# A decoder layer with three token mixers: five of the dilated mixer's seven projections per head computed as seven-block products

## The chip, the cores and the metric

One core of a Trainium2 chip runs the whole program. The metric is device time in microseconds of one execution. A core's engines are called PE (TensorE, with its weight load PEld), ACT (ScalarE), DVE (VectorE), POOL (GpSimd) and SP (SyncE, which issues most transfers). Each works through its own list in order; a semaphore holds an instruction until what it needs is there.

## The reference, cut to what matters

`x` has 512 tokens of width 2048. One projection of the normalised and modulated input `u` gives all columns of the layer, and a part of them feeds the dilated mixer (C): three groups of eight heads, 128 columns per head and group, and a gate `c_z`.

```
u = rms_norm(x, norm_w) * (1.0 + scale) + shift
proj = u @ w_in                       # 512 x 2048 times 2048 x 23552
for g, (w, d) in enumerate(((128, 1), (512, 4), (2048, 16))):
    s = q[g] @ k[g].T * 128 ** -0.5   # a window of w, every d-th token
    o[g], lse[g] = softmax(s) @ v[g], logsumexp(s)
o_c = sum(softmax(lse)[g] * o[g])     # per token and head
y_c = (o_c * silu(c_z)) @ w_proj_c    # A (differential) and B (retention) alike
merged = sigmoid(g_a) * y_a + sigmoid(g_b) * y_b + sigmoid(g_c) * y_c
out = rms_norm(x + gate * (merged @ w_out), final_norm_w)
```

## The kernel before, in words

**Products.** A float32 product is made of three matmuls on a high and a low part of each operand (`mm3`, L157 to L160). A plain projection of 128 output columns (`proj`, L162) loads two weight halves of 512 KB on SP (`w_load`, L130, tile `wr`, three buffers), splits each by a copy on ACT (L146, `wh`) and a subtraction on DVE (L147, `wl`), and runs 16 row blocks times 3 matmuls, 48 in all, of 128x512.

**Stages.** The start phase forms the modulation, `u`, and some gate columns; POOL does the low parts of those weights there (L278). Then comes the phase of seven-block products (L496 to L698), then the eight heads of mixer C (L942 to L974), the C gate phase, mixers A and B with theirs, and the output product.

**The phase of seven-block products.** A unit (`unit_jobs`, L555) is the product of `u` with 1024 weight columns, cut into 2x2 blocks and computed with seven block products in place of eight. It has 14 jobs: P1 (2), P2 (2), R3 (2) and eight sum jobs. A job loads one 1 MB raw tile `xr` (SP, two jobs ahead, three buffers), splits it (`xh` on ACT, L506; `xl` on DVE, L507), forms sums on DVE in the sum jobs (L592), and multiplies (`block_mul`). For values a job has 24 matmuls of 128x512. For the gates (`fm=True`, output with features on partitions) it has 48 of 128x256. The results are collected in the steps `keep` (L574, ACT copies P1 to tile `p1` and R3 to tile `r3`), `p2_done` (L580, DVE writes tile `c`), `done_z` (L610), `done_s` (L616 and L617) and `done_rest`. Tiles `c`, `r3`, `s` and `z` have one buffer each. Each is written to DRAM by a DMA that POOL issues (`put_values`, L643; `put_gates`, L655, behind a sigmoid on ACT), so the same tile of the next unit waits for that DMA to land.

There are nine units: three of C's values, A's and B's values, and four of gates: 126 jobs. PE, ACT and DVE instructions of this phase are kept in program order (`pin`, L152). POOL's instructions are not: a scheduler places them.

**The heads of C.** Each head runs seven plain projections (q and k for each group, and z). Scores, softmax, transposes and values are placed between their two halves (`mid=`). Values come back from DRAM for two heads at a time (`v_load`, L210, into the `wr` buffers). The softmax sums cross DRAM (`bounce`), and POOL reads back the weights `wtb`. POOL also forms nine columns of gate bias (`gate_bias_load`, L707): per column four loads of 256 KB into one buffer `bw` (L711), each with a multiplication by the shift and two or three additions (L713 to L719). PE adds up the partitions (L724).

Of the kernel before, what the change touches and what calls it, by code (L numbers as in the profile page):

```python
# [64 lines left out]
def hybrid_kernel(ctx, tc, x, c, w_in, w_pa, w_pb, w_pc, w_out, w_ada, b_ada, norm_w, lam,  # L65
# [32 lines left out]


# [34 lines left out]

    def w_half(src, k0, c0, rot=False, tiles=None, low=dve):

        r, h, l = tiles or w_load(src, k0, c0)
# [7 lines left out]
        else:  # L145
            act.copy(h, r)  # L146
            low.tensor_sub(l, r, h.bitcast(F32))  # L147
        return h, l

    pinned = [False]  # L150

    def pin(instr):  # L152

        if pinned[0]:
            tc.keep_in_program_order(instr)
# [40 lines left out]
    def split_pairs(pool, tag, src):  # L196

        t = pool.tile([P, 4, 2, P], F32R, tag=tag, name=tag)
        act.copy(t[:, :, 0, :], src)
        dve.tensor_sub(t[:, :, 1, :], src, t[:, :, 0, :].bitcast(F32))  # L200
        return t
# [448 lines left out]
    def put_gates(g, b0):  # L650
        def put(t, half, cc):
            def f():
# [6 lines left out]


    units = [unit_jobs(w_in, c0, put_values(unit), early=unit == 3)
             for unit, c0 in ((2, C_V), (3, C_V + 1024), (4, C_V + 2048), (0, A_V), (1, B_V))]
    units += [unit_jobs(w_in, g + b0 * P, put_gates(g, b0), fm=True) for g in (G_A, G_B) for b0 in (0, 8)]
    jobs = units[1][0] + units[0][0] + units[0][1] + units[1][1]
# [26 lines left out]
    pinned[0] = False  # L691
    for f in later:
        f()
    for f in deferred:
        f()
    wx_es.close()
# [3 lines left out]
    wp_es, wp = open_pool("wp2", "left", reuse_waits="tile")  # L700
# [4 lines left out]


    def gate_bias_load(pool, db):  # L707
        br = pool.tile([P, P], F32, tag="br", name="br", bufs=2)
        for q in range(4):
            r = pool.tile([P, 4, P], F32, tag="bw", name="bw", bufs=1)  # L710
            nc.gpsimd.dma_start(out=r, in_=w_in[q * 512:(q + 1) * 512, G_C + db * P:G_C + (db + 1) * P]  # L711
                              .rearrange("(j p) c -> p j c", p=P))
            nc.gpsimd.tensor_mul(r, r, sh[:, q * 4:q * 4 + 4].unsqueeze(2).broadcast_to([P, 4, P]))  # L713
            nc.gpsimd.tensor_add(r[:, 0:2, :], r[:, 0:2, :], r[:, 2:4, :])
            if q == 0:
                nc.gpsimd.tensor_add(br, r[:, 0, :], r[:, 1, :])
            else:
                nc.gpsimd.tensor_add(r[:, 0, :], r[:, 0, :], r[:, 1, :])
                nc.gpsimd.tensor_add(br, br, r[:, 0, :])  # L719
        return br  # L720
# [87 lines left out]
    def bias_step():  # L808
        while bias_open:
            gate_bias_sum(*bias_open.pop(0))  # L810
# [520 lines left out]
```

## Time and profile before

| | us |
|---|---|
| median of three runs | 2669.22 (2666.35 to 2669.69) |
| the profiled execution | 2663.64 |
| its span | 2661.9 |
| start phase, up to the first seven-block job | 0 to 238.6 |
| seven-block products, nine units | 238.6 to 961 |
| C's first head, up to the next turn | 961 to 1055.2 |
| one C head after that | 84.7 |
| what follows the C heads | from 1647.6 |

The span runs from the first to the last instruction of the profiled execution. In the rows further down, a timeline row has the start in us, the duration in us, the engine, the line in the kernel, the operation, out<-in, sizes, and in brackets how long the engine had been idle and what released it. A row "x36 | 287.0, 1271" of the groups gives the count, the busy us and the mean ns of one. A window row has the stretch, its length, and for PE, PEld, DVE, ACT and POOL the busy us with the number of instructions, then PE's granted clock, DMA share and GB/s. A row of the DMA issues gives count, KB each, and us from issue to landing.

### The profile page before, as it was taken

The numbers are of one execution on the slowest core, as the hardware profiler recorded it, in microseconds if no ns is written. First come the engines' busy times: TensorE is split into PE (matmuls) and PEld (weight loads), VectorE is DVE, ScalarE is ACT, GpSimd is POOL, SyncE is SP. The second block draws the span as 40 slices with busy tenths as digits, with TensorE's granted clock in tenths as the row PEclk, the third lists the DMA queues.
The fourth block names the chain that finished last, engine by engine and source line by source line (L and its number), as shares of the span: only waits on it lengthen the run. The fifth ranks groups of instructions, "written<-read, shape, count | busy, mean of one in ns | idle before, by whom it ended". The sixth has DMA issues, their size and how long they took to land.

```text
span 2661.9 us, 33296 instructions
## 1 busy us (share of the span) xinstructions
PE 2568.5 (96%) x13091; PEld 2184.6 (82%) x13091; DVE 1689.0 (63%) x2427; ACT 1058.6 (40%) x1431; POOL 269.6 (10%) x271
## 2 busy tenths in 40 slices
PE   6999999999999999999999999999999989999898
PEld 5777778888999988888888888788888768878778
DVE  7994888777778754444443444357667457676674
ACT  4233433333334433233333333246666235653222
POOL 3332000000000024122214200000000000000000
PEclk9999999999999999999999999999999999999999
DMA  9776666666666655344445443542333563336862
GB/s 345 252 273 227 231 208 226 225 221 214 197 207 220 208 154 147 96 119 120 114 119 123 106 121 109 175 142 82 93 88 92 171 194 104 98 99 210 299 222 103
DMA packets 414017, 449.47 MB, mean 169 GB/s; under 512 B 24786, under 2 KB 308132, under 8 KB 412708
## 3 DMA queue, kind: packets, MB, share of 16 engines
q1 hardware_dynamic: 384388, 396.91, 47.6%
q0 software_dynamic: 9760, 33.59, 4.2%
q10 hardware_dynamic: 19712, 16.85, 1.9%
q8 instruction: 102, 1.67, 0.3%
q14 instruction: 55, 0.45, 0.1%
HBM read 406.86 MB, written 40.44 MB: 168 GB/s over the span
## 4 chain that ended last, share of the span: by engine, by line
PE 74%; DVE 11%; DMA 8%; ACT 3%; issue 2%; SPq 0%; POOL 0%; ACTq 0%; DVEq 0%
PE pj L158 15%; PE pj L160 15%; PE pj L159 15%; PE at L159 8%; PE at L160 8%; PE at L158 8%; DVE acc L318 3%; DMA gpr<-part 2%; DMA gwa<-in_w_ada_dram 1%; DVE xl L507 1%; DMA gsg<-g 1%; DMA xr<-in_w_in_dram 1%; DMA part<-gsg 1%; DMA xr<-ud 1%; DVE xr L592 1%
## 5 line engine op out<-in xcount | busy, mean ns | idle before, releaser
L158 PE MATMUL pj<-uh,wh 128*128 128x512 f32 x1552 | 611.9, 394 | 7.1 <-ACT wh L146 4.8
L160 PE MATMUL pj<-uh,wl 128*128 128x512 f32 x1552 | 608.0, 392 | 7.3 <-DVE wl L144 4.6
L159 PE MATMUL pj<-ul,wh 128*128 128x512 f32 x1552 | 606.7, 391 | 0.0
L147 DVE TENSOR_TENSOR wl<-wr,wh 128x1024 fp32r<-128x1024 f32 x226 | 287.0, 1271 | 392.0 <-ACT wh L146 364.6
L146 ACT CAST wh<-wr 128x1024 fp32r<-128x1024 f32 x228 | 239.2, 1051 | 516.7 <-PE pj L159 365.7
L506 ACT CAST xh<-xr 128x2048 fp32r<-128x2048 f32 x126 | 240.7, 1910 | 365.0 <-PE at L160 152.5
L507 DVE TENSOR_TENSOR xl<-xr,xh 128x2048 fp32r<-128x2048 f32 x126 | 288.8, 2292 | 125.4 <-ACT xh L506 124.6
L160 PEld LDWEIGHTS pj<-uh,wl 128*128 128x128 f32 x1552 | 292.5, 188 | 70.3 <-DVE wl L144 5.5
L158 PEld LDWEIGHTS pj<-uh,wh 128*128 128x128 f32 x1552 | 293.0, 189 | 65.1 <-ACT wh L146 5.0
L159 PEld LDWEIGHTS pj<-ul,wh 128*128 128x128 f32 x1552 | 292.8, 189 | 58.1
L592 DVE TENSOR_TENSOR xr<-xr 128x512 f32<-128x512 f32 x288 | 198.8, 690 | 12.3 <-DMA xr<-in_w_in_dram 5.1
L158 PE MATMUL at<-yh,wh 128*128 128x512 f32 x336 | 131.8, 392 | 5.9 <-DVE gsg L777 5.0
L159 PE MATMUL at<-yl,wh 128*128 128x512 f32 x336 | 131.5, 391 | 0.0
L160 PE MATMUL at<-yh,wl 128*128 128x512 f32 x336 | 131.5, 391 | 0.0
L160 PE MATMUL at<-fh,xl 128*128 128x256 f32 x384 | 108.9, 284 | 0.7 <-DVE xl L507 0.7
L158 PE MATMUL at<-fh,xh 128*128 128x256 f32 x384 | 108.7, 283 | 0.0
L159 PE MATMUL at<-fl,xh 128*128 128x256 f32 x384 | 108.7, 283 | 0.0
L158 PE MATMUL at<-wh,mh 128*128 128x512 f32 (+1 forms) x256 | 93.1, 369 | 6.2 <-DVE res L1252 3.8
L159 PE MATMUL at<-wl,mh 128*128 128x512 f32 (+1 forms) x256 | 94.9, 371 | 0.2
L160 PE MATMUL at<-wh,ml 128*128 128x512 f32 (+1 forms) x256 | 94.5, 369 | 0.0
L278 POOL TENSOR_TENSOR wl<-wr,wh 128x896 fp32r<-128x896 f32 x32 | 77.3, 2421 | 136.5 <-ACT wh L277 127.3
L159 PE MATMUL at<-xl,fh 128*128 128x512 f32 x224 | 88.8, 396 | 2.1 <-DVE xl L507 1.8
(419 smaller groups left out, 5035.4 us busy)
## 6 DMA issues: line engine op xcount, KB each, us to landing
wr<-in_w_in_dram SPq DMA_DIRECT2D x196, 512.0 KB, 3.9
xr<-in_w_in_dram SPq DMA_DIRECT2D x144, 512.0 KB, 4.5
xr<-in_w_in_dram SPq DMA_DIRECT2D x54, 1024.0 KB, 5.1
wa<-in_w_ada_dram SPq DMA_DIRECT2D x20, 1024.0 KB, 9.1
wr<-in_w_out_dram SPq DMA_DIRECT2D x32, 512.0 KB, 4.6
gwa<-in_w_ada_dram SPq DMA_DIRECT2D x32, 512.0 KB, 4.8
wr<-in_w_in_dram SPq DMA_DIRECT2D x32, 448.0 KB, 6.3
wb<-in_w_ada_dram SPq DMA_DIRECT2D x12, 1024.0 KB, 9.3
```

What stands on the lines that cost most here:

```text
L146: act.copy(h, r)
L147: low.tensor_sub(l, r, h.bitcast(F32))
L158: pin(nc.tensor.matmul(ps, lhsT=ah, rhs=bh, start=start, stop=False))
L159: pin(nc.tensor.matmul(ps, lhsT=ah, rhs=bl, start=False, stop=False))
L160: pin(nc.tensor.matmul(ps, lhsT=al, rhs=bh, start=False, stop=stop))
L278: nc.gpsimd.tensor_sub(l, r, h.bitcast(F32))
L318: dve.scalar_tensor_tensor(out=acc, in0=wa[:, j, :], scalar=sc[:, k:k + 1], in1=acc, op0=ALU.mult, op1=ALU.add)
L506: pin(act.copy(h, r))
L507: pin(dve.tensor_sub(l, r, h.bitcast(F32)))
L592: pin(dve.tensor_add(r[:, o, :], r[:, o, :], r[:, a, :]))
```

## The change

Of the seven projections of a C head, q1, k1, q2, k2 and q3 are computed for all heads as five more units of the seven-block kind (features on partitions, as the gates), and written to DRAM (`qk_dram`) by `put_raw`. A's and B's value units move behind them, so the phase has 14 units, 196 jobs. k3 and z stay plain projections.

- A head reads its five operands back from DRAM in `raw_load` tiles: two operands of 256 KB per tile, tag `wr`, the three buffers that the weight halves use as well. Values are now read per head. `head_inputs` of the next head stands behind z; `head_values` stands behind k3.
- The head's other work stands around the two projections: the previous head's turn, the first scores and scores(1) at the middle of k3; the previous head's values behind k3; the first turn and scores(2) at the middle of z.
- `wtb` has a tile of its own, and its DMA is issued right after the write of the sums.
- The gate bias leaves the C heads. It is cut into 72 pieces (`bias_piece`: a load of 128 KB into one buffer `bw`, a multiplication, one or two additions, all on POOL), whose code stands one per job in jobs 16 to 87 of the seven-block phase. The nine columns go to DRAM (`br_dram`), and SP reads one per head (L838).
- The two weight halves of the first k3 are split between the last steps of the seven-block phase.

```diff
+    QK = [C_Q, C_K, C_Q + 1024, C_K + 1024, C_Q + 2048]
+    qk_dram = [dram.tile([8, P, S], F32, tag=f"qk{i}", name=f"qk{i}") for i in range(len(QK))]
+    br_dram = dram.tile([NF + NM, P, P], F32, tag="brd", name="brd")
...
+        if tiles is not None and len(tiles) == 2:
+            return tiles
...
-            act.copy(h, r)
-            low.tensor_sub(l, r, h.bitcast(F32))
+            pin(act.copy(h, r))
+            pin(low.tensor_sub(l, r, h.bitcast(F32)))
...
+    def put_raw(dst):
+        def put(t, half, cc):
+            b = cc // P
+            nc.gpsimd.dma_start(out=dst[b:b + 4, :, half * 256:half * 256 + 256].rearrange("b p t -> p b t"),
+                                in_=t.rearrange("p q (a t) -> p (q a) t", a=2))
+        return put
...
+    def bias_piece(n):
+        db, q = divmod(n, 8)
+        if q == 0:
+            bias_tiles[db] = wxp.tile([P, P], F32, tag="br", name="br")
+        br = bias_tiles[db]
+        r = wxp.tile([P, 2, P], F32, tag="bw", name="bw")
+        nc.gpsimd.dma_start(out=r, in_=w_in[q * 256:(q + 1) * 256, G_C + db * P:G_C + (db + 1) * P]
+                          .rearrange("(j p) c -> p j c", p=P))
+        nc.gpsimd.tensor_mul(r, r, sh[:, q * 2:q * 2 + 2].unsqueeze(2).broadcast_to([P, 2, P]))
+        if q == 0:
+            nc.gpsimd.tensor_add(br, r[:, 0, :], r[:, 1, :])
+        else:
+            nc.gpsimd.tensor_add(r[:, 0, :], r[:, 0, :], r[:, 1, :])
+            nc.gpsimd.tensor_add(br, br, r[:, 0, :])
+        if q == 7:
+            nc.gpsimd.dma_start(out=br_dram[db], in_=bias_tiles.pop(db))
...
-             for unit, c0 in ((2, C_V), (3, C_V + 1024), (4, C_V + 2048), (0, A_V), (1, B_V))]
+             for unit, c0 in ((2, C_V), (3, C_V + 1024), (4, C_V + 2048))]
     units += [unit_jobs(w_in, g + b0 * P, put_gates(g, b0), fm=True) for g in (G_A, G_B) for b0 in (0, 8)]
+    units += [unit_jobs(w_in, c0, put_raw(dst), fm=True) for c0, dst in zip(QK, qk_dram)]
+    units += [unit_jobs(w_in, c0, put_values(unit)) for unit, c0 in ((0, A_V), (1, B_V))]
...
-    pinned[0] = False
+        if 2 * HJ <= i < 2 * HJ + 8 * (NF + NM):
+            bias_piece(i - 2 * HJ)
+    wx_es.close()
+    wp_es, wp = open_pool("wp2", "left", reuse_waits="tile")
+    loads = [w_load(w_in, half * 1024, C_K + 2048) for half in range(2)]
+    entry = []
+    for tiles in loads:
+        entry.append(w_half(w_in, 0, 0, tiles=tiles))
+        later.pop(0)()
     for f in later:
         f()
-    for f in deferred:
-        f()
-    wx_es.close()
+    pinned[0] = False
...
-    def gate_bias_load(pool, db):
-        br = pool.tile([P, P], F32, tag="br", name="br", bufs=2)
-        for q in range(4):
-            r = pool.tile([P, 4, P], F32, tag="bw", name="bw", bufs=1)
-            nc.gpsimd.dma_start(out=r, in_=w_in[q * 512:(q + 1) * 512, G_C + db * P:G_C + (db + 1) * P]
-                              .rearrange("(j p) c -> p j c", p=P))
-            nc.gpsimd.tensor_mul(r, r, sh[:, q * 4:q * 4 + 4].unsqueeze(2).broadcast_to([P, 4, P]))
-            nc.gpsimd.tensor_add(r[:, 0:2, :], r[:, 0:2, :], r[:, 2:4, :])
-            if q == 0:
-                nc.gpsimd.tensor_add(br, r[:, 0, :], r[:, 1, :])
-            else:
-                nc.gpsimd.tensor_add(r[:, 0, :], r[:, 0, :], r[:, 1, :])
-                nc.gpsimd.tensor_add(br, br, r[:, 0, :])
-        return br
...
-    bias_todo, bias_open = list(range(NF + NM)), []
+    bias_todo = list(range(NF + NM))
     def bias_step():
-        while bias_open:
-            gate_bias_sum(*bias_open.pop(0))
-        bias_more()
-    def bias_more():
         if bias_todo:
             db = bias_todo.pop(0)
-            bias_open.append((db, gate_bias_load(cp, db)))
+            br = cp.tile([P, P], F32, tag="br", name="br", bufs=2)
+            nc.sync.dma_start(out=br, in_=br_dram[db])
+            gate_bias_sum(db, br)
...
+            ctx_["wtb"] = cp.tile([P, 2, S], F32, tag="wtb", name="wtb")
+            nc.gpsimd.dma_start(out=ctx_["wtb"], in_=ctx_["bounce"].partition_broadcast(P))
...
-            wtb = cp.tile([P, 2, S], F32, tag="e23", name="wtb")
-            nc.gpsimd.dma_start(out=wtb, in_=ctx_["bounce"].partition_broadcast(P))
-            ctx_["p"], ctx_["wtb"] = ps, wtb
+            ctx_["p"] = ps
...
+    def raw_load(*srcs):
+        r = wp.tile([P, 2, S], F32, tag="wr", name="wr", bufs=3)
+        for i, (src, view) in enumerate(srcs):
+            nc.sync.dma_start(out=view(r[:, i, :]), in_=src)
+        return r
...
+    def head_inputs(hd):
+        got = []
+        for g in range(2):
+            r = raw_load((qk_dram[2 * g][hd], same), (qk_dram[2 * g + 1][hd], same))
+            got.append((split(cp, "q", r[:, 0, :], scale=dh_scale, view=perm if g else None, bufs=2),
+                        split_pairs(cp, "kc", perm(r[:, 1, :]) if g else tiles4(r[:, 1, :]), bufs=2)))
+        return got
+    def head_values(hd):
+        srcs = [(v_dram[2][:, hd * P:(hd + 1) * P].rearrange("(t p) c -> p t c", p=P), tiles4)]
+        srcs += [(v_dram[2 + g][:, hd * P:(hd + 1) * P].rearrange("(i r) c -> i r c", r=4), tiles4) for g in (1, 2)]
+        rs = [raw_load((qk_dram[4][hd], same), srcs[0]), raw_load(*srcs[1:])]
+        q3 = split(cp, "q", rs[0][:, 0, :], scale=dh_scale, view=perm, bufs=2)
+        vs = []
+        for g in range(3):
+            src = tiles4(rs[(g + 1) // 2][:, (g + 1) % 2, :])
+            vh = cp.tile([P, NT, P], F32R, tag=f"v{g}h", name="vh")
+            vl = cp.tile([P, NT, P], F32R, tag=f"v{g}l", name="vl")
+            act.copy(vh, src)
+            dve.tensor_sub(vl, src, vh.bitcast(F32))
+            vs.append((vh, vl))
+        return q3, vs
...
     left = [None, None]
+    inputs = head_inputs(0)
     for hd in range(8):
-        bias_step()
         e1 = cp.tile([P, NT, 256], F32, tag="e1", name="e1")
         st = cp.tile([P, 4, 4], F32, tag="st", name="st", bufs=2)
-        q = split(cp, "q", proj(C_Q + hd * P, mid=left[0]), scale=dh_scale)
-        kc = split_pairs(cp, "kc", proj(C_K + hd * P, mid=left[1]).rearrange("p (r i) -> p r i", r=4))
         p0 = [cp.tile([P, 4, 256], F32R, tag=f"p0{x}", name=f"p0{x}") for x in "hl"]
         e23 = cp.tile([P, 4, 256], F32, tag="e23", name="e23")
         first_scores, first_turn, scores, turn, values, weigh, finish = c_head(hd, e1, e23, st, p0)
-        cq, ck = C_Q + hd * P, C_K + hd * P
-        ps = proj(cq + 1024, mid=lambda: first_scores(*q, kc))
-        q2 = split(cp, "q", ps, scale=dh_scale, view=perm)
-        ps = proj(ck + 1024, mid=first_turn)
-        kc2 = split_pairs(cp, "kc", perm(ps))
-        ps = proj(cq + 2048, mid=lambda: scores(1, *q2, kc2))
-        q3 = split(cp, "q", ps, scale=dh_scale, view=perm)
-        kc3 = split_pairs(cp, "kc", perm(proj(ck + 2048)))
-        if hd == 4:
-            bias_more()
-        if hd % 2 == 0:
-            vs = [v_load(cp, 2 + g, hd * P, f"v{g}", strided=g > 0) for g in range(3)]
-        sz = silu(cp, proj(C_Z + hd * P, mid=lambda: scores(2, *q3, kc3)))
+        (q1, kc1), (q2, kc2) = inputs
+        def opening(turn_left=left[0], q1=q1, kc1=kc1, q2=q2, kc2=kc2):
+            if turn_left is not None:
+                turn_left()
+            first_scores(*q1, kc1)
+            scores(1, *q2, kc2)
+        ps = proj(C_K + 2048 + hd * P, tiles=entry or (None, None), mid=opening)
+        entry = None
+        if left[1] is not None:
+            left[1]()
+        kc3 = split_pairs(cp, "kc", perm(ps), bufs=2)
+        q3, vs = head_values(hd)
+        def closing(q3=q3, kc3=kc3):
+            first_turn()
+            scores(2, *q3, kc3)
+        sz = silu(cp, proj(C_Z + hd * P, mid=closing))
+        bias_step()
+        if hd < 7:
+            inputs = head_inputs(hd + 1)
...
```

Most lines of `unit_jobs` and the helpers keep their text and move by six (L643 becomes L649, L574 becomes L580, L147 becomes L160, L132 becomes L136).

POOL is the engine whose list changes most. In the first rows of the seven-block phase, before: the last L278 of the start phase, then the transfers of the first units (`p1d` and `p1_...` are one unit's P1 put aside and fetched again, `vd2` and `vd3` are C's values in DRAM, `c`, `r3`, `s` and `z` the four result tiles):

```order
L278 TENSOR_TENSOR wl_1714<-wr_1712,wh_1713 128x896
L583 DMA p1d_72<-p1_1942 128x1024
L643 DMA vd3_78<-c_2024 128x2x512
L643 DMA vd2_77<-c_2190 128x2x512
L602 DMA p1_2657<-p1d_72 128x1024
L643 DMA vd2_77<-r3_2266 128x2x512
L643 DMA vd2_77<-s_2587 128x2x512
```

POOL now, around the write of the first tile `c` (`bw` is a piece's load and work tile, `br` the column that it is added to):

```order
L683 DMA bw_3025<-in_w_in_dram 128x2x128
L685 TENSOR_TENSOR bw_3025<-bw_3025,sh_98 128x256
L689 TENSOR_TENSOR bw_3025<-bw_3025 128x128
L690 TENSOR_TENSOR br_2870<-br_2870,bw_3025 128x128
L683 DMA bw_3071<-in_w_in_dram 128x2x128
L649 DMA vd3_78<-c_2030 128x2x512
L685 TENSOR_TENSOR bw_3071<-bw_3071,sh_98 128x256
L689 TENSOR_TENSOR bw_3071<-bw_3071 128x128
```

Where the write of `c` was the second transfer behind the start phase, 14 loads of pieces and the work of 13 now stand ahead of it. Before, the third unit's writes follow the second's with nothing between them:

```order
L643 DMA vd3_78<-z_2918 128x2x512
L643 DMA vd4_79<-c_3061 128x2x512
L643 DMA vd4_79<-r3_3137 128x2x512
L643 DMA vd4_79<-s_3453 128x2x512
L643 DMA vd4_79<-z_3418 128x2x512
L643 DMA vd0_75<-c_3561 128x2x512
```

POOL now, at the last piece, some 240 rows further (`vd4` is the third unit of C's values, `g17408` the first of A's gates):

```order
L683 DMA bw_6549<-in_w_in_dram 128x2x128
L685 TENSOR_TENSOR bw_6549<-bw_6549,sh_98 128x256
L689 TENSOR_TENSOR bw_6549<-bw_6549 128x128
L690 TENSOR_TENSOR br_6102<-br_6102,bw_6549 128x128
L692 DMA brd_85<-br_6102 128x128
L649 DMA vd4_79<-r3_3230 128x2x512
L649 DMA vd4_79<-s_3616 128x2x512
L649 DMA vd4_79<-z_3552 128x2x512
L661 DMA g17408_70<-c_3811 128x4x256
```

All 72 pieces stand ahead of the third unit's write of `r3`, although the code places the later ones among the gate units and the units behind them. Between these two places, the write of the first unit's `r3` (`vd2_77<-r3_2272`) stands behind 40 loads, that of the second's (`vd3_78<-r3_2656`) behind 57, the third's `c` (`vd4_79<-c_3143`) behind 61. The list of ACT, which is kept in program order, at the tile that is written next into the buffer of `r3_3230`, now:

```order
L512 CAST xh_3894<-xr_3819 128x2048
L580 COPY r3_3946<-at_3832 128x512
L580 COPY r3_3946<-at_3833 128x512
L512 CAST xh_3962<-xr_3887 128x2048
L512 CAST xh_4034<-xr_3955 128x2048
```

Behind the copies of `r3_3946`, which reuse the buffer that the DMA `vd4_79<-r3_3230` reads, stand the splits of all later jobs.

SP's list of a C head before is a run of weight halves, with three reads of values for every second head:

```order
L132 DMA wr_8233<-in_w_in_dram 128x8x128
L132 DMA wr_8263<-in_w_in_dram 128x8x128
L215 DMA wr_8296<-vd2_77 128x4x256
L215 DMA wr_8302<-vd3_78 128x4x256
L215 DMA wr_8308<-vd4_79 128x4x256
L132 DMA wr_8315<-in_w_in_dram 128x8x128
```

And now, one whole head (each `wr` number is one tile):

```order
L968 DMA wr_12650<-qk0_80 128x512
L968 DMA wr_12650<-qk1_81 128x512
L968 DMA wr_12660<-qk2_82 128x512
L968 DMA wr_12660<-qk3_83 128x512
L136 DMA wr_12676<-in_w_in_dram 128x8x128
L136 DMA wr_12767<-in_w_in_dram 128x8x128
L968 DMA wr_12841<-qk4_84 128x512
L968 DMA wr_12841<-vd2_77 128x4x128
L968 DMA wr_12844<-vd3_78 128x4x128
L968 DMA wr_12844<-vd4_79 128x4x128
L136 DMA wr_12864<-in_w_in_dram 128x8x128
L136 DMA wr_12941<-in_w_in_dram 128x8x128
```

Fourteen weight halves per head have become four, and the rest of the eight tiles are operands and values; all eight go through the three `wr` buffers in this order.

28 lines of the change are left out of this document (16 added, 12 removed).

## Prediction

> **What bounds the kernel now.** I read the page first, then the table of windows by stage, then timelines of PE, ACT, DVE and POOL around the places that the change touches. The page's first part gives the load of each engine.
>
> ```profile
> PE 2568.5 (96%) x13091; PEld 2184.6 (82%) x13091; DVE 1689.0 (63%) x2427; ACT 1058.6 (40%) x1431; POOL 269.6 (10%) x271
> ```
>
> PE is busy 96% of the span and POOL 10%. By stage (the value units from 280, the gate units from 630, two C heads of 84.7 us):
>
> ```profile
> 280.00:630.00 350.00, 343.54 (x1492) 281.58 (x1492) 287.83 (x285) 129.39 (x81) 11.98 (x17) 0.99 0.64 217
> 630.00:961.00 331.00, 330.29 (x2721) 328.74 (x2720) 253.20 (x243) 129.09 (x86) 11.93 (x16) 1.00 0.61 203
> 1055.20:1139.90 84.70, 84.70 (x410) 71.30 (x409) 34.99 (x65) 28.63 (x47) 17.63 (x22) 1.00 0.40 107
> ```
>
> PE never waits in a C head (84.70 of 84.70), hardly in the gate units (330.29 of 331.00), and 6.5 us in 350 of value units. So taking matmuls away shortens the kernel, as long as nothing else becomes late. DVE is second in the seven-block phase: 287.83 of 350. POOL does 12 us of work in either of the first two windows, which is only the issuing of transfers.
>
> **The matmuls removed and added.** A matmul's own duration overlaps the next, so its cost is the spacing of starts. 128x512 first, then 128x256:
>
> ```profile
> 1099.91 0.39 PE L159 MATMUL pj<-ul,wh 128*128 128x512 f32 x1
> ...
> 1104.89 0.40 PE L160 MATMUL pj<-uh,wl 128*128 128x512 f32 x1
> ```
> ```profile
> 940.81 0.28 PE L158 MATMUL at<-fh,xh 128*128 128x256 f32 x1
> ...
> 942.97 0.28 PE L158 MATMUL at<-uh,xh 128*128 128x256 f32 x1
> ```
>
> Between the first two lie 22 steps: 4.98 / 22 = 0.2264 us. Between the second two lie 18: 2.16 / 18 = 0.120 us. A plain projection is 48 x 0.2264 = 10.9 us; five per head and eight heads are 40 of them, 435 us less on PE. A feature-major unit has 14 jobs of 48, 672 x 0.120 = 80.6 us; five are 403 us more. **The change takes 32 us off PE.** By the Trainium skill ("TensorE: Matmul & The Clock Gate", Back-to-back issue gap) a matmul of N columns takes N / 2.4 GHz and about 2.5 ns, which is 109 and 216 ns; the saving would be 47 us by it. The traced spacings are 10% and 5% longer, and they are what I use.
>
> **The entry into the C heads.** Before, PE stops where the first projection's weights are split only after the last job:
>
> ```profile
> 961.21 0.28 PE L160 MATMUL at<-uh,xl 128*128 128x256 f32 x1
> 966.26 0.79 PE L158 MATMUL pj<-uh,wh 128*128 128x512 f32 x1 [4.77 <-ACT wh L146]
> ```
>
> The two weight halves now lie between the last collecting steps, so I take 4 of these 4.8 us as saved. The bound is zero, if the collecting steps delay them instead.
>
> **The gate bias on POOL.** This decides the case. The pieces' code stands one per job, but POOL's list has 14 loads of pieces ahead of the write of the first `c`, 40 ahead of the first `r3`, 57 ahead of the second, and all 72 ahead of the third (`vd4_79<-r3_3230`). POOL works in order, so those writes leave when the pieces ahead are done, whatever job PE has reached. Today they leave as soon as DVE has the tile:
>
> ```profile
> 267.87 0.73 POOL L643 DMA_DIRECT2D vd<-c  x1 [13.94 <-DVE c L580]
> 355.40 0.71 POOL L643 DMA_DIRECT2D vd<-r  x1 [6.86 <-DVE r L617]
> ```
>
> The next tile in the same buffer waits for the landing, which one ACT copy already shows (4 us, then the split behind it in ACT's list):
>
> ```profile
> 358.78 1.07 ACT L574 COPY r<-pj 128x512 f32<-128x512 f32 x2 [3.95 <-DMA vd<-r]
> 359.74 1.92 ACT L506 CAST xh<-xr 128x2048 fp32r<-128x2048 f32 x1
> ```
>
> What stands behind a waiting copy on ACT is the split `xh` of every later job. DVE's subtraction and then PE follow within a job or two.
>
> A piece's time comes from the pieces of twice its size in a C head. Undisturbed, and then beside DVE's splits and values:
>
> ```profile
> 1018.89 0.79 POOL L711 DMA_DIRECT2D bw<-in_w_in_dram  x1 [0.29 <-POOL br L719]
> 1022.36 1.03 POOL L713 TENSOR_TENSOR bw<-bw,sh 128x512 f32<-128x512 f32 x1 [2.68 <-DMA bw<-in_w_in_dram]
> 1023.47 0.73 POOL L714 TENSOR_TENSOR bw<-bw 128x256 f32<-128x256 f32 x1
> 1024.28 0.46 POOL L718 TENSOR_TENSOR bw<-bw 128x128 f32<-128x128 f32 x1
> 1024.82 0.46 POOL L719 TENSOR_TENSOR br<-br,bw 128x128 f32<-128x128 f32 x1
> 1025.58 0.79 POOL L711 DMA_DIRECT2D bw<-in_w_in_dram  x1 [0.29 <-POOL br L719]
> ```
> ```profile
> 1155.23 1.04 POOL L713 TENSOR_TENSOR bw<-bw,sh 128x512 f32<-128x512 f32 x1 [1.42 <-DMA bw<-in_w_in_dram]
> 1156.35 0.73 POOL L714 TENSOR_TENSOR bw<-bw 128x256 f32<-128x256 f32 x1
> 1157.16 0.79 POOL L718 TENSOR_TENSOR bw<-bw 128x128 f32<-128x128 f32 x1
> 1158.03 0.79 POOL L719 TENSOR_TENSOR br<-br,bw 128x128 f32<-128x128 f32 x1
> ```
>
> From issue to the multiplication it takes 3.47 us for 256 KB. A piece loads 128 KB. Its multiplication is of 256 elements, as the 0.73 us of L714, or less. It has two additions of 0.46 us, 0.08 between each, and 0.29 before the next issue. With the same load that is 3.47 + 0.73 + 2 x (0.08 + 0.46) + 0.29 = 5.6 us. With a load shorter by a quarter (an estimate; half the bytes, but the same issue and completion) and a multiplication of 0.6 it is 4.6 us. With additions of 0.79 us beside DVE it is 6.3 us. **I take 5.5 us**, the undisturbed row nearly as it stands: smaller load, some contention. The ends 4.6 and 6.3 go into the range.
>
> POOL is free of the start phase here:
>
> ```profile
> 228.86 2.13 POOL L278 TENSOR_TENSOR wl<-wr,wh 128x896 fp32r<-128x896 f32 x1 [6.85 <-ACT wh L277]
> ```
>
> That is at 231.0. The steps that wait stand, before, at these times (the first `c` of a reused buffer on DVE, then the `r3` copies of the third and fourth unit on ACT; the second's is quoted above):
>
> ```profile
> 289.51 1.28 DVE L580 TENSOR_TENSOR c<-p,at 128x512 f32<-128x512 f32 x2
> ```
> ```profile
> 440.61 1.27 ACT L574 COPY r<-at 128x512 f32<-128x512 f32 x2 [3.19 <-PE at L160]
> ```
> ```profile
> 517.17 1.27 ACT L574 COPY r<-at 128x512 f32<-128x512 f32 x2 [3.20 <-PE at L160]
> ```
>
> And a write takes this long to land:
>
> ```profile
> vd<-c POOLq DMA_DIRECT2D x5, 512.0 KB, 4.1
> vd<-r POOLq DMA_DIRECT2D x5, 512.0 KB, 3.4
> ```
>
> The first `c` may leave after 13 pieces and two issues: 231 + 71.5 + 1.5 + 0.7 + 4 = 309, so DVE waits some 19 us at 289.5. The second unit's `r3` waits for the first's, behind 39 pieces: 231 + 214 + 8 of transfers issued + 3.4 = 457, against 358.8: 98 us late in all. The third unit's: 231 + 56 x 5.5 + 13 + 3.4 = 555, against 440.6: 115 late. The fourth unit's (now the first gate unit's): 231 + 72 x 5.5 = 627, nine writes of `brd` and eleven other transfers at 0.73 (14.6), 3.4 to land: 645, against 517.2. **So 128 us are lost by then**, the four waits being one delay that grows. Behind that place POOL only issues transfers, and the units of gates, operands and values run as today's do. After the last wait PE restarts below its full clock, as it does at 966.26 (0.79 where 0.39 is usual), which costs another 2 us; at the earlier waits that is covered by POOL's pace. At 4.6 us a piece the loss is 231 + 331.2 + 18 - 517.2 = 63; at 6.3 it is 185.
>
> **The C heads anew.** On PE a head has 84.7 - 5 x 10.9 = 30.3 us of work. Through the three `wr` buffers now go eight tiles per head: four weight halves, two tiles of operands, two with q3 and values. The rows for a tile:
>
> ```profile
> wr<-in_w_in_dram SPq DMA_DIRECT2D x196, 512.0 KB, 3.9
> ```
> ```profile
> L147 DVE TENSOR_TENSOR wl<-wr,wh 128x1024 fp32r<-128x1024 f32 x226 | 287.0, 1271 | 392.0 <-ACT wh L146 364.6
> L146 ACT CAST wh<-wr 128x1024 fp32r<-128x1024 f32 x228 | 239.2, 1051 | 516.7 <-PE pj L159 365.7
> ```
>
> Load, copy and subtraction are 3.9 + 1.05 + 1.27 = 6.2 us in which the buffer is taken. Three of eight tiles in one buffer are 19 us, which fits in 30.3. But ACT and DVE take the tiles in order among softmax and values, and where five in a row depend on one another it is 31 us and more. The load of one head on DVE falls only a little below its 35 us of before: weight splits of ten halves (12.7 us) go, and five splits of projections stay as splits of operands. So DVE has some 23 us in 30.3. I put 1.5 us of waiting on each head, **12 us** in all, between 0 and 30. The sums' way through DRAM must also be covered within a head:
>
> ```profile
> bounce<-st ACTq DMA_DIRECT2D x8, 4.0 KB, 11.4
> wtb<-bounce POOLq DMA_DIRECT2D x8, 512.0 KB, 5.0
> ```
>
> The writing takes 11.4 us and the read of `wtb`, now issued at once, 5.0. Together they are 16 of a head's 30 us, so I count nothing. POOL's bias work (17.6 us per head) leaves the heads, where it hid beside PE; that is worth nothing. The 20 writes of `put_raw` come on POOL behind the pieces, with 80 us of PE per four of them: nothing.
>
> **The sum**, against the profiled execution of 2663.6 us (span 2661.9 and 1.7 outside it): 2663.6 - 32 - 4 + 128 + 2 + 12 = **2769**. The median of before, 2669.2, lies 5.6 us above that execution; a measurement of this kernel tells 0.2%, some 5 us, from no change.
>
> **Rivals.** The first one needs the fastest landing of POOL's loads, from the view of tile `bw`:
>
> ```profile
> DMA to landing us min/median/max: 3.3/4.2/9.1
> ```
>
> *POOL keeps ahead (the other side).* If the pieces run so fast that the writes are late by no more than the 36 us saved, the kernel is faster. The loss is 231 + 72q + 18 - 517; it is 22 us (leaving room for the heads' 12 and the 2) at q = 4.0 us per piece. At 3.7 the loss is near zero and the time 2663.6 - 36 + 0 to 10, about 2632. It would need the load, with issue, to take 2 us where 256 KB take 3.47. For it speaks that the load is half as large; against it that the fastest of POOL's 36 loads landed after 3.3 us, and that the copy of `r3` is fixed behind all 72. Chance 0.07, with 0.03 for the strip around no change.
>
> *POOL and DVE shut each other out.* Beside DVE an addition grew from 0.46 to 0.79 us, and DVE from 1.27 to 2.15:
>
> ```profile
> 1152.76 2.15 DVE L147 TENSOR_TENSOR wl<-wr,wh 128x1024 fp32r<-128x1024 f32 x1 [3.61 <-ACT wh L146]
> ```
>
> In the value units DVE is busy 82% with operations of up to 2.29 us that read two tiles. If each of a piece's three operations waits half of such an operation, a piece takes 5.0 + 3 x 0.9 = 7.7 us while DVE works, and 4.8 while DVE itself waits. From 231 to 517 the phase without its waits takes 286 us; in that 37 pieces are done, and the other 35 take 168 us. The loss is 168 + 18 = 186, and the time 2827. The Trainium skill ("SBUF — State Buffer", Who interferes with whom) speaks for this, and so against the change: it says that DVE with two inputs in SBUF and a reading GpSimd operation exclude each other for the whole instruction. The longer rows here agree with it in direction, but only some of POOL's operations show it, because DVE was busy only 40% of a head. Chance 0.15.
>
> *The heads become bound by their buffers.* If all eight tiles come in one chain with ACT and DVE, a head takes 36 us, the heads lose 45 in place of 12, and the time is 2802. The eightfold use of three buffers speaks for it, the 19 us against it. Chance 0.10.
>
> **How the numbers follow.** The likeliest case (0.65) gives 2769, with 2663.6 - 36 + 63 + 2 + 0 = 2693 and 2663.6 - 36 + 185 + 2 + 12 = 2827 at its ends. The two slower rivals lie at 2802 and 2827. I give 2700 to 2830. Faster by over 0.2% has 0.07, within it 0.03, slower 0.90. That the change doesn't do what it says is in the likeliest case itself: "one piece per job" is not what POOL's list holds.
>
> **What would show it.** The trace of after should show POOL's L683 to L690 back to back from 231 to about 640, with no idle time but the loads; DVE's `c` near 290 waiting some 20 us for `vd<-c`; ACT's `r3` copies released by `vd<-r`, the last near 645; PE idle some 128 us between 290 and 650 and hardly at all from there to the C heads; units of 80.6 us; heads of 30 to 33 us; and no gap of 4.8 us at their entry. I am wrong if POOL's pieces come spaced by job, if a piece takes under 4 us, or if the heads take over 35.

## The result, and the profile after

The changed kernel takes 2867.4 us (median of four, 2863.5 to 2872.5) against 2668.05 before: 1.075 times as long, 95% interval 1.073 to 1.077. The forecast was 2769, between 2700 and 2830. The direction was right, and of the 199 us lost it had 100. The first part of the page of after, and of its 40 slices those of PE, POOL and PE's granted clock:

```profile
span 2863.3 us, 36858 instructions
PE 2576.8 (90%) x14531; PEld 2249.6 (79%) x14531; DVE 1907.7 (67%) x2654; ACT 1130.8 (39%) x1453; POOL 346.7 (12%) x408
PE   7899635798999999999998878899999989999898
POOL 3344545541000000000000000000000000000000
PEclk9999877998999999999998889899999999999999
```

PE is as busy as before in sum (2577 us against 2568), in a span 201 us longer. It has two holes: slices 5 to 10, where POOL works, and slices 22 to 26, the C heads, where POOL does almost nothing. The windows of after give their size (units before and behind the end of POOL's pieces, then seven C heads):

```profile
280.00:660.00 380.00, 250.44 (x1203) 209.28 (x1202) 213.54 (x200) 93.71 (x62) 190.31 (x275) 0.83 0.50 168
660.00:1364.00 704.00, 701.66 (x5772) 698.84 (x5772) 538.14 (x514) 264.74 (x171) 25.60 (x34) 1.00 0.62 207
1552.60:1839.60 287.00, 231.73 (x1184) 193.68 (x1182) 157.16 (x397) 141.30 (x268) 18.17 (x20) 0.88 0.46 113
```

PE is idle for 129.6 of 380 us in the first, for 2.3 of 704 in the second. In seven heads it is idle for 55 of 287 us, and its clock is at 0.88 there.

For all kernels I cut the span at four starts of matmuls: the first and the last on `xh` or `xl` (the phase begins and ends), the next matmul behind it (the heads begin), and the first of the last head's turn (the rest begins). The profiled execution gives each row; the same code can take some us more or less in it (the phase of e2 and e7 has the code of after's). The loss of the phase is its length less before's 722.6 and, where the five units are in it, less their 403.2 us of matmuls.

| | phase | its loss | heads | rest | span |
|---|---|---|---|---|---|
| before | 722.6 | 0 | 681.4 | 1014.2 | 2661.9 |
| after | 1265.2 | 139.4 | 336.0 | 1023.7 | 2863.3 |
| e5, before with the pieces | 857.7 | 135.1 | 681.4 | 1020.3 | 2804.2 |
| e1, POOL in program order | 1178.3 | 52.5 | 339.4 | 1025.4 | 2782.6 |
| e3, two half-size buffers | 1254.1 | 128.3 | 341.0 | 1024.6 | 2858.3 |
| e9, loads without the work | 1244.5 | 118.7 | 336.3 | 1024.0 | 2843.6 |
| e2, sums written as rows | 1264.5 | 138.7 | 285.2 | 1021.2 | 2811.1 |
| e7, the same, placed later | 1273.6 | 147.8 | 272.1 | 1014.5 | 2799.2 |
| e6, e7's sums, piece every 2nd job | 1134.0 | 8.2 | 271.4 | 1019.2 | 2664.0 |
| e11, e6 with fewer small buffers | 1131.3 | 5.5 | 271.1 | 1031.7 | 2673.7 |
| e10, e11 and a fourth buffer | 1129.2 | 3.4 | 250.9 | 1030.4 | 2650.5 |

After against before: 403 us of units and 139 of waiting and slow clock in the phase, 5 saved at the entry (no gap between the last job and the first k3), 345 saved in the heads, 9.5 more in the rest. The heads lost 435 us of matmuls and gained 90 us of waiting and slow clock.

**The phase.** ACT's copies of `r3` and DVE's first `c` in after, the places that were to wait:

```profile
315.97 1.28 DVE L586 TENSOR_TENSOR c<-p,at 128x512 f32<-128x512 f32 x2 [11.79 <-DMA vd<-c]
```
```profile
461.38 1.07 ACT L580 COPY r<-pj 128x512 f32<-128x512 f32 x2 [78.43 <-DMA vd<-r]
...
559.98 1.07 ACT L580 COPY r<-at 128x512 f32<-128x512 f32 x2 [22.07 <-DMA vd<-r]
...
656.33 1.07 ACT L580 COPY r<-at 128x512 f32<-128x512 f32 x2 [20.88 <-DMA vd<-r]
```

Each is released by the landing of a write that POOL issued (`DMA vd<-`). They come 26, 103, 119 and 139 us later than before; forecast were 19, 98, 115 and 128. The view of the pieces' tile shows how long they took:

```profile
L683 POOL DMA_DIRECT2D bw<-in_w_in_dram x72: 702/743/886, 230.4 to 647.7; - x72
L685 POOL TENSOR_TENSOR bw<-bw,sh x72: 602/604/2563, 233.3 to 650.5; 128x256 f32<-128x256 f32 x72
L689 POOL TENSOR_TENSOR bw<-bw x63: 446/462/2392, 238.8 to 651.2; 128x128 f32<-128x128 f32 x63
```

72 pieces from 230.4 to 652.2 are 5.86 us each with the 19 other transfers that POOL issued among them. These took 12.7 us, so a piece alone took 5.7, where the forecast has 5.5 and counts the other transfers apart. While the phase waits, a piece takes 4.6 (401.05 to 405.66), and beside DVE an operation of 0.60 us can last four times as long:

```profile
401.05 0.74 POOL L683 DMA_DIRECT2D bw<-in_w_in_dram  x1 [0.29 <-POOL br L690]
403.70 0.60 POOL L685 TENSOR_TENSOR bw<-bw,sh 128x256 f32<-128x256 f32 x1 [1.91 <-DMA bw<-in_w_in_dram]
...
405.66 0.74 POOL L683 DMA_DIRECT2D bw<-in_w_in_dram  x1 [0.30 <-POOL br L690]
```
```profile
295.62 2.26 POOL L685 TENSOR_TENSOR bw<-bw,sh 128x256 f32<-128x256 f32 x1 [1.93 <-DMA bw<-in_w_in_dram]
297.96 1.32 POOL L689 TENSOR_TENSOR bw<-bw 128x128 f32<-128x128 f32 x1
```

The group of the multiplications gives both parts of what a piece takes more, on average, than those 4.6 us, the operation (0.79 us for 0.60) and the wait for the load (177.1 us for 71 loads, 2.5 each, for 1.9):

```profile
L685 POOL TENSOR_TENSOR bw<-bw,sh 128x256 f32<-128x256 f32 x72 | 56.9, 791 | 180.9 <-DMA bw<-in_w_in_dram 177.1 <-DVE xl L513 3.8
```

All of the pieces' operations together took 142 us, where at 0.60 and 0.45 us they would take 104; the loads' waits took 177 where 1.9 us each would be some 135. So the operations beside DVE and the slower loads each added about 40 us (estimates).

**The heads.** What PE waited for there, in all, times, longest:

```profile
PE pj L164 <- ACT wh L159: 45.6, 8, 7.7
PE at L750 <- DVE gpr L945: 14.7, 5, 3.9
```

So once a head, PE waits 6 us for a weight split on ACT. ACT's timeline in one head shows where ACT was:

```profile
1644.98 0.37 ACTq L870 DMA_DIRECT2D bounce<-st  x1
1645.93 0.57 ACT L205 CAST kc<-pj 128x512 fp32r<-128x512 f32 x1
1646.40 0.63 ACT L944 COPY gpr<-at 128x256 f32<-128x256 f32 x1
1658.31 0.63 ACT L197 ACTIVATE qh<-wr 128x512 fp32r<-128x512 f32 x1 [11.27 <-DMA wr<-qk]
```

It stood 11.27 us before the split of the next head's q, waiting for its load; everything else on ACT, the next weight split too, stood behind. The issues of 1645 to 1660 (KB, and us to landing), and the window behind the issue of the loads:

```profile
wr<-qk SPq DMA_DIRECT2D x2, 256.0 KB, 11.0
bounce<-st ACTq DMA_DIRECT2D x1, 4.0 KB, 11.5
```
```profile
1647.30:1656.50 9.20, 9.20 (x50) 7.85 (x49) 1.10 (x2) 0.00 (x0) 0.00 (x0) 1.00 0.24 22
```

The two loads (issued 1647.3) land 11 us later, where such a load's median is 3.1 us. The write of the first group's sums, issued 2.3 us before them, is 4 KB in elements of 4 bytes, and until it has landed at 1656.5 only 22 GB/s move. The packets by queue, of 1645 to 1647.3 and then of 1647.3 to 1656.5 (q10 is ACT's queue, q1 SP's; packets, MB, share of 16 engines):

```profile
q10 hardware_dynamic: 1040, 0.00, 20.3%
```
```profile
q1 hardware_dynamic: 104, 0.20, 23.6%
```

All 1040 packets of the write are recorded before the loads are issued; from then until the write has landed, only SP's queue has packets, and few. The Trainium skill ("DMA: Bandwidth & Descriptors", Queues, rings and completion order) says that each transfer engine takes turns between the queues, a packet at a time. By these records there was nothing left in ACT's queue to take turns with, so that rule does not explain the slow loads. That the write causes them is shown by e2 below; what holds them after its packets are recorded stays open. Before has the same write in each head, and its trace had a warning: the weight load issued behind it at 1344.4 (its view, by source line and window) landed this late,

```profile
L132 SPq DMA_DIRECT2D wr<-in_w_in_dram x1: 368/368/368, 1344.4 to 1344.4; - x1
...
DMA to landing us min/median/max: 9.5/9.5/9.5
```

but there six other projections of 10.9 us covered it.

### The profile page after: what moved, and what is told of

Read it like the earlier page. It is cut to its first block, busy times and chain, and to the rows that moved or that the text cites. A ratio compares the mean times of both kernels' runs of the same rounds, so it can differ in the third digit from the quotient of the medians.

```text
span 2863.3 us, 36858 instructions
## 1 busy us (share of the span) xinstructions
PE 2576.8 (90%) x14531; PEld 2249.6 (79%) x14531; DVE 1907.7 (67%) x2654; ACT 1130.8 (39%) x1453; POOL 346.7 (12%) x408
## 5 line engine op out<-in xcount | busy, mean ns | idle before, releaser
L513 DVE TENSOR_TENSOR xl<-xr,xh 128x2048 fp32r<-128x2048 f32 x196 | 452.3, 2308 | 319.9 <-ACT xh L512 318.8
L164 PE MATMUL pj<-uh,wh 128*128 128x512 f32 x912 | 369.7, 405 | 46.7 <-ACT wh L159 43.5
L166 PE MATMUL pj<-uh,wl 128*128 128x512 f32 x912 | 365.9, 401 | 5.3 <-POOL wl L160 2.6
L165 PE MATMUL pj<-ul,wh 128*128 128x512 f32 x912 | 364.2, 399 | 0.0
L160 DVE TENSOR_TENSOR wl<-wr,wh 128x1024 fp32r<-128x1024 f32 x146 | 178.4, 1223 | 162.2 <-ACT wh L159 161.5
L165 PEld LDWEIGHTS pj<-ul,wh 128*128 128x128 f32 x912 | 177.1, 194 | 35.1
L164 PE MATMUL at<-uh,xh 128*128 128x256 f32 x576 | 164.0, 285 | 13.3 <-ACT r L580 13.3
L166 PEld LDWEIGHTS at<-fh,xl 128*128 128x128 f32 x864 | 166.5, 193 | 1.3 <-DVE xl L513 1.3
L164 PEld LDWEIGHTS at<-fh,xh 128*128 128x128 f32 x864 | 166.7, 193 | 0.0
L165 PEld LDWEIGHTS at<-fl,xh 128*128 128x128 f32 x864 | 166.5, 193 | 0.0
L165 PE MATMUL at<-ul,xh 128*128 128x256 f32 x576 | 163.9, 285 | 0.0
L166 PE MATMUL at<-uh,xl 128*128 128x256 f32 x576 | 163.8, 284 | 0.0
## 6 DMA issues: line engine op xcount, KB each, us to landing
xr<-in_w_in_dram SPq DMA_DIRECT2D x84, 1024.0 KB, 5.1
wa<-in_w_ada_dram SPq DMA_DIRECT2D x20, 1024.0 KB, 9.7
wb<-in_w_ada_dram SPq DMA_DIRECT2D x12, 1024.0 KB, 9.8
```

Source lines behind the costliest of these rows:

```text
L160: pin(low.tensor_sub(l, r, h.bitcast(F32)))
L164: pin(nc.tensor.matmul(ps, lhsT=ah, rhs=bh, start=start, stop=False))
L165: pin(nc.tensor.matmul(ps, lhsT=ah, rhs=bl, start=False, stop=False))
L166: pin(nc.tensor.matmul(ps, lhsT=al, rhs=bh, start=False, stop=stop))
L513: pin(dve.tensor_sub(l, r, h.bitcast(F32)))
```

## The experiments

Theory Q: in the phase, the writes stand behind the pieces in POOL's list. Rival L: POOL's and DVE's operations shut each other out. Theory B: in the heads, the write of the sums in 4-byte elements holds the loads behind it. Rival R: eight tiles through three buffers, with ACT and DVE in order, make the heads late by themselves.

**e5, the pieces alone.** The kernel before with `bias_piece` of the changed kernel, called in the same jobs, and its `bias_step`:

```diff
+        if 2 * HJ <= i < 2 * HJ + 8 * (NF + NM):
+            bias_piece(i - 2 * HJ)
```

> The kernel before, with its gate bias alone formed as in the changed kernel (72 pieces in the seven-block phase, read back by SP in the heads); no new units, and the C heads as before. If the pieces' place alone makes the phase late, the loss of 139 us is here too: 2668 + 139 = 2807, between 2795 and 2820. If it takes the new units or their writes to make it, the time is 2668 to 2690.

Measured: 2805.4 against 2667.3 on the same chip, 138 us more; the phase lost 135.1 and the heads nothing. The pieces' place alone makes the loss of the phase. With 135.1 of 139.4 us there without them, the new units have hardly a part in it.

**e1, the order.** All of POOL's transfers and operations in the phase are kept in program order, as PE's, ACT's and DVE's are (`put_values` as an example; likewise the other writes and the whole of `bias_piece`):

```diff
-            nc.gpsimd.dma_start(out=v_dram[unit][half * 256:half * 256 + 256, cc:cc + 512]
+            pin(nc.gpsimd.dma_start(out=v_dram[unit][half * 256:half * 256 + 256, cc:cc + 512]
```

> Everything that POOL does in the seven-block phase is kept in program order (pieces and writes); nothing else differs from the changed kernel. Theory Q (the writes stand behind the pieces in POOL's list): the 139 us lost in the phase go but for what a piece of 5.9 us exceeds a value job of 5.4, some 10 to 30 us; 2867 - 139 + 20 = 2750, between 2738 and 2760. Theory L (POOL's and DVE's operations shut each other out): the same operations meet the same DVE work, about 1.5 us late in each of 72 jobs, so some 100 us stay: 2830.

Measured: 2777.6, a loss of 52.5 us in the phase: most of the 139 went, but more stayed than Q said (10 to 30) and less than L did (some 100). The waits of PE from 238 to 700, one of ACT's from 238 to 860, and a window name it:

```profile
PE at L164 <- ACT r L580: 17.7, 2, 14.0
PE pj L165 <- DVE xl L513: 7.3, 4, 2.8
```
```profile
ACT r L580 <- DMA g<-r: 52.1, 3, 22.2
```
```profile
600.00:680.00 80.00, 64.37 (x521) 63.67 (x520) 51.72 (x48) 22.50 (x14) 37.80 (x53) 0.91 0.58 191
```

The longest wait is still `r3` for its write. The pieces run from 292.7 to 832.6, 7.5 us each, and a gate job takes 80.64 / 14 = 5.8. One piece per job is more than POOL can do, so it falls behind, and the writes with it. So the slow pieces and the writes behind them act at once here; e6 separates them.

**e6, half the density, and the sums.** A piece in every second job, POOL in order as in e1, and the sums written as in e7 below:

```diff
-        if 2 * HJ <= i < 2 * HJ + 8 * (NF + NM):
-            bias_piece(i - 2 * HJ)
+        if 2 * HJ <= i < 2 * HJ + 2 * 8 * (NF + NM) and i % 2 == 0:
+            bias_piece((i - 2 * HJ) // 2)
```

> The changed kernel with both mended: POOL in program order with a piece in every second job (jobs 16 to 158), and the first group's sums turned on PE behind the previous head's values and written as 8 rows of 512 bytes. Theory: no backlog on POOL is left, a piece of 6 to 7.5 us fits in two jobs of 11, so the phase loses under 15 us of its 139 (what DVE and POOL take from each other); no load is held in the heads, which take 247 to 255 us for eight instead of 336 (30.3 each on PE). 2867 - 139 + 8 - 86 = 2650, between 2638 and 2662, so faster than before. If three buffers (theory R) hold the heads, they stay at 34 us and more, and the time is 2680.

Measured: 2663.6 against 2665.5, a ratio of 0.9995 (0.998 to 1.001): no change from before. The phase came out as expected, with a loss of 8.2. The same 72 pieces stand beside DVE, spread over twice the jobs, and PE is busy throughout the stretch of 600 to 680. The multiplications, in the whole phase, took longer than in after:

```profile
600.00:680.00 80.00, 80.00 (x664) 80.00 (x663) 62.77 (x56) 30.77 (x22) 25.84 (x32) 0.99 0.63 214
```
```profile
L685 POOL TENSOR_TENSOR bw<-bw,sh 128x256 f32<-128x256 f32 x72 | 69.5, 966 | 257.7 <-DMA bw<-in_w_in_dram 257.7
```

All of the pieces' operations took 188 us here and 142 in after, and still the phase lost 8. So with no write late behind them, what POOL and DVE take from each other costs the kernel 8 us at most, and L falls as a cause by itself. In after the slower operations do add to the time of the pieces that stand ahead of the writes; no run keeps that list and takes away only the slowing, so its share of the 139 is not measured. The heads did not come out: 271 us where 247 to 255 was expected.

**e3, faster pieces (failed).** Pieces of half the size in two buffers, to load one beside the work on the other; the rest as in the changed kernel:

```diff
-        r = wxp.tile([P, 2, P], F32, tag="bw", name="bw")
+        for k in (2 * q, 2 * q + 1):
+            r = wxp.tile([P, P], F32, tag="bw", name="bw", bufs=2)
```

> The bias pieces are cut in two (64 KB, one multiplication and one addition of 128x128) and have two buffers of half the size, so that a load runs beside the operations of the one before; the order of POOL's list is as in the changed kernel. Theory Q: only the pace of the pieces sets the loss; at 2.0 to 2.2 us per half, 4.0 to 4.4 per piece, it is 231 + 72 x 4.2 + 18 - 517 = 34 us instead of 139: 2762, between 2745 and 2780. Theory L: POOL's operations beside DVE are as many or more, the loss stays over 110: 2840 and more.

Measured: 2860.8, a loss of 128.3. The 144 halves took 2.81 us each (231 to 635), 5.6 per piece: hardly faster.

**e9, the loads alone.** The multiplication and all but nine of the full additions are left out:

```diff
-        nc.gpsimd.tensor_mul(r, r, sh[:, q * 2:q * 2 + 2].unsqueeze(2).broadcast_to([P, 2, P]))
...
-            nc.gpsimd.tensor_add(r[:, 0, :], r[:, 0, :], r[:, 1, :])
-            nc.gpsimd.tensor_add(br, br, r[:, 0, :])
+            nc.gpsimd.tensor_add(br[:, 0:1], br[:, 0:1], r[:, 0, 0:1])
```

> The changed kernel with the 72 loads of the pieces in their places but nearly no work on them (one addition of 128x128 per column of the bias, else one element; the multiplication by the shift and the sums are left out, so the C gate's bias is wrong). Theory Q: the pace alone counts; at 3.2 to 3.6 us a piece the longest lag is that of the second unit's r3, 231 + 39 x 3.4 + 8 + 3.4 = 375 against 358.8, so 10 to 25 us are lost instead of 139: 2867 - 139 + 16 = 2744, between 2735 and 2755. If the traffic of the loads itself or a fixed place in the list made the phase late, 100 us and more stay.

Measured: 2847.0, a loss of 118.7, against my 10 to 25. While the phase waits a piece does take 3.2 us (549.57 to 552.74 below), but the list had not stayed: it holds 50 loads ahead of the first `r3` instead of 40, and 72 ahead of the second instead of 57. In e3 these are 84 and 122 halves. POOL's timeline at the first `r3` write in after, e3 and e9, and at the second in e9:

```profile
457.12 0.74 POOL L683 DMA_DIRECT2D bw<-in_w_in_dram  x1 [0.29 <-POOL br L690]
457.86 0.73 POOL L649 DMA_DIRECT2D vd<-r  x1
```
```profile
454.19 0.58 POOL L684 DMA_DIRECT2D bw<-in_w_in_dram  x1 [0.30 <-POOL br L690]
...
455.12 0.76 POOL L649 DMA_DIRECT2D vd<-r  x1
```
```profile
447.44 0.74 POOL L683 DMA_DIRECT2D bw<-in_w_in_dram  x1 [0.29 <-POOL br L686]
448.17 0.73 POOL L649 DMA_DIRECT2D vd<-r  x1
...
549.57 0.72 POOL L683 DMA_DIRECT2D bw<-in_w_in_dram  x1 [0.29 <-POOL br L688]
552.27 0.18 POOL L688 TENSOR_TENSOR br<-br,bw 128x1 f32<-128x1 f32 x1 [1.98 <-DMA bw<-in_w_in_dram]
552.74 0.72 POOL L683 DMA_DIRECT2D bw<-in_w_in_dram  x1 [0.29 <-POOL br L688]
553.46 0.73 POOL L649 DMA_DIRECT2D vd<-r  x1
```

In three kernels with pieces of different length, the first `r3` leaves within 10 us of the same time, 448 to 458, against 355 before. The shorter the piece, the more of them the list puts ahead. As if by a reckoning of its own: up to 355.4 it has room for 39 pieces at (355 - 231) / 39 = 3.2 us (an estimate) where a piece took 5.8, and in e9 for 49 at 2.5 where it took 4.4. "The pace alone" was wrong as an expectation because the list is made anew for each kernel.

**e2 and e7, the sums.** The 128x8 tile of the first group's sums is turned on PE and leaves as 8 rows of 512 bytes. In e2 this stands where the write stood, in e7 behind the previous head's values:

```diff
-            nc.scalar.dma_start(out=bounce.rearrange("s (a p) -> p s a", p=P), in_=st1)
+            tp = at()
+            nc.tensor.transpose(tp[0:2 * NT, 0:P], st1.rearrange("p s a -> p (s a)"), ident)
+            st1t = cp.tile([P, P], F32, tag="st1t", name="st1t")[0:2 * NT, :]
+            dve.tensor_copy(st1t, tp[0:2 * NT, 0:P])
+            nc.scalar.dma_start(out=bounce.rearrange("s (a p) -> (s a) p", p=P), in_=st1t)
```

> Only the write of the first group's sums in a C head differs from the changed kernel: the 128x8 tile is turned on PE and copied by DVE, and goes to DRAM as 8 rows of 512 bytes instead of 1024 elements of 4 bytes. Theory B (that write holds every load issued behind it until it has landed): the load of q and k behind it lands in some 3 us instead of 11, a head falls from 41.7 to 33 to 35 us, and the time from 2867 to 2800 to 2817. Theory R (eight tiles through three buffers, with ACT and DVE in order): heads stay within 1 us of 41.7, 2857 to 2870.

> The changed kernel with the sums of the first group turned on PE behind the previous head's values (not right behind the scores, where PE waited 27 us for the exponentials in eight heads) and written as 8 rows; its POOL as it was. Theory B: the heads fall from 336 to 247 to 255 us, 2867 - 85 = 2782, between 2775 and 2795. Theory R: they stay at 285, as with the earlier place, 2814.

Measured: e2 2814.4, its heads 285.2 instead of 336.0, as B said. ACT's wait for q, 64.5 us in six heads before, is down to this, and PE waits at the turn that I had added, for the exponentials whose sums it turns:

```profile
ACT qh L197 <- DMA wr<-qk: 5.1, 4, 2.1
```
```profile
PE at L871 <- ACT e L866: 27.2, 8, 5.9
```

e7 takes that wait away: heads of 272.1, where B said 247 to 255 and R 285. Its time, 2803.6, is above the 2795 of B, also because its phase, which the edit does not touch, lost 8 us more than after's. So B holds for 64 of the 90 us, and something else has the rest. (In e6, with the same write, ACT's wait for q is 18.1 us in all and 3.2 at most, so the loads are not wholly free of waiting.)

**e8, the same in the kernel before.**

> The kernel before, with the first group's sums turned on PE and written as 8 rows of 512 bytes. There the held load (9.5 us in one case) lies beside seven projections with 10.9 us of matmuls each, and PE never waited: no change, 2667 within 4 us. If the held loads cost time there too, it is faster by 10 or more.

Measured: 2662.7 against 2665.5, 0.9993 (0.998 to 1.000), heads 681.4 as before: the held load cost nothing there.

**e10 and e11, a fourth buffer.** Both are e6 with one buffer for three small tiles and a smaller tile of ones; e10 also gives every second `raw_load` a buffer of its own:

```diff
-        r = wp.tile([P, 2, S], F32, tag="wr", name="wr", bufs=3)
+        r = cp.tile([P, 2, S], F32, tag="rw", name="rw") if own else wp.tile([P, 2, S], F32, tag="wr", name="wr", bufs=3)
```

> The mended kernel (POOL in order, a piece every second job, sums written as rows) with a fourth 4 KB buffer in the C heads: the second tile of operands and the tile of two value blocks have a buffer of their own, the other six tiles share the three. To make room, the tiles for the turned sums, the lows and the bias columns have one buffer. Theory R in its smaller form (the three buffers still cost the heads 3 us each: a weight half lands 1 to 3 us late): heads 271 -> 250 to 258, and 2664 - 17 = 2647, between 2640 and 2655, 0.4 to 0.9% faster than before. If what is left is the order on ACT and DVE, heads stay at 268 to 274, and the time at 2660 to 2667.

> The same tiles with one buffer, but without the fourth buffer: the control for the run beside it. 2664 within 4 us, heads 268 to 276, if the tiles that gave up a buffer held nothing up.

Measured: e10 2649.1 against 2669.05, 0.9925 (0.991 to 0.994); e11 2667.9, 0.9999. The heads fall from 271.1 to 250.9, 30.8 each. The window of e10's eight heads:

```profile
1369.20:1620.10 250.90, 248.61 (x1349) 210.48 (x1348) 191.84 (x474) 166.77 (x317) 22.69 (x25) 1.00 0.55 164
```

PE is busy all but 2.3 us, at full clock. R was right for 20 us, once B was out of the way.

## Why the prediction was wrong

- **The matmuls, -32: right.** A unit's period in after is 80.66 us (for example from 877.4 to 958.1, the copies of P1), the forecast 80.6; a head's matmuls take 30.8 us in e10, the forecast 30.3.
- **The entry, -4: right.** The gap of 4.8 us is gone, and the first k3 matmul follows the last job after 0.2 us.
- **POOL, +128: right in cause, 11 us too small.** It was 139. The piece took 5.7 us instead of 5.5, and the four waits came in their places. e5 shows the loss with the pieces alone, and e1 with e6 that it needs the order: the same work with the writes in their places costs 8. The 5.5 was near partly by luck. It was taken as an undisturbed piece with "some contention", but an undisturbed piece takes 4.6, by the same sum a loss of 63, and the slower operations and loads brought it to 5.7. That the list itself underrates a piece's time stood in no step; e3 and e9 point to it.
- **The restart, +2: right in kind, within the 139.** PE's first matmul behind the 75.6 us wait takes 0.79 us, as at the entry of before. Behind the last wait the starts of 128x256 matmuls lie 0.21 us apart instead of 0.12 until 666.0, some 3 us for 35 of them (an estimate).
- **The C heads, +12 between 0 and 30: wrong; it was 90.** This is the step that put the forecast out. Two sentences failed. "Together they are 16 of a head's 30 us, so I count nothing" took the write of the sums for a latency of its own chain. It was that too, but for 11 us the loads issued behind it are also late, and one of these is now next in ACT's list: 64 us (e7). And "I put 1.5 us of waiting on each head" was too little for three buffers: 20 us, 2.5 per head (e10 against e11). The other 6 are not traced one by one. I had quoted the row of 11.4 us, and had the weight load of 9.5 us been looked up beside it, the first would have shown.
- **The rest, nothing forecast: 9.5 us more.** No edit touches it; it was between 1 us shorter (e8) and 17.5 longer (e11) than before's in the experiments. This is not settled.
- **The rivals.** The heads bound by their buffers had the right place, 36 us a head; they took 42, mostly by another mechanism. POOL and DVE shutting each other out would have given 186 in the phase; it was 139, with about 40 us of slower operations in the pieces and e6 losing 8 with more of them. That POOL keeps ahead did not happen: a load landed in 2.7 us, faster than the 3.3 I held against it, but a piece with both additions did not get under 4.6.

The sum with the measured terms is 2663.6 - 32 - 5 + 139 + 90 + 9.5 = 2865, and the profiled execution took 2865.0. The terms are stretches of its own span, so that the sum closes is no proof of any of them.

## What to carry to other kernels

- Where some engines' instructions are pinned and one engine's are not, read that engine's list before trusting "one per step" in the code. How much it puts ahead changed here with the length of the pieces, so that the delay hardly did; the writes behind them are late, and so is every engine that reuses their buffers.
- A stage shortened to a third shows every latency that the old length covered: look in the trace for the slowest transfers there (here 11.4 and 9.5 us), and ask which loads are issued behind them and who waits for these in order.

## What the runs showed of the hardware

- A write of 4 KB in 1024 elements of 4 bytes took 11.5 us to land, though its 1040 packets were recorded within the first 2.3 us, and in the last 9.2 us only 22 GB/s moved. As 8 rows of 512 bytes it hardly delayed the loads behind it (ACT's wait for them went from 64.5 to 5.1 us in e2).
- POOL's operation of 0.60 us took up to 2.56 us beside DVE (2.26 in the rows above). The Trainium skill ("SBUF — State Buffer", Who interferes with whom) has DVE with two inputs in SBUF and a reading GpSimd operation exclude each other for the whole instruction, and the rows agree. An addition of 0.45 us that starts 0.47 us behind one of DVE's splits ends 0.31 us behind that split's end, 2.38 us after its own start:

```profile
320.72 2.38 POOL L690 TENSOR_TENSOR br<-br,bw 128x128 f32<-128x128 f32 x1
```
```profile
320.25 2.54 DVE L513 TENSOR_TENSOR xl<-xr,xh 128x2048 fp32r<-128x2048 f32 x1
```

With nothing late behind the pieces, it cost the kernel at most 8 us in 72 of them (e6).
